# Sliding windows by DMA: thirteen staged batches, one doubled store for each, and the last 15 windows of a copy on GpSimd's ring

## The chip, the core and the metric

The kernel runs on one core of one Trainium2 chip. It uses no compute engine: all of its work is DMA transfers, which the core's 16 DMA engines carry out. Three of the core's queues can issue them: SyncE's (SP), ScalarE's (ACT) and GpSimd's (POOL). A transfer that is issued is cut into packets; each DMA engine holds a ring of waiting packets for each issuing queue. The metric is the device time of the whole program in microseconds (us), as the median of several runs. One further run was profiled; its trace gives the spans, the queues and the single packets.

## The reference

A float32 array `x` of 32 batches x 4096 rows x 256 columns is cut into overlapping windows of 64 rows, one every 32 rows. Each batch gives 127 windows, and each window is written out whole:

```python
n_windows = (length - window_size) // stride + 1      # 127
result = np.zeros((batch, n_windows, window_size, dim), dtype=np.float32)
for i in range(n_windows):
    start = i * stride
    result[:, i] = x[:, start:start + window_size].copy()
```

A block of 32 rows is 32 KB (32,768 bytes), and a batch has 128 such blocks. A window is two neighbouring blocks, 64 KB. Every block but the first and the last of a batch therefore stands in the output twice: as the second half of window p - 1 and as the first half of window p. In the output these two places are neighbours: half-windows 2p - 1 and 2p.

## The kernel before, in words

Batches go one of two ways.

A **direct** batch (20 of 32) is copied from DRAM to DRAM by SP's queue, `copy` (lines 93 to 99): three transfers of 80, 32 and 15 windows (`COPY_PARTS`, line 16). The second number of each pair says into how many packets a 64 KB window is cut: 4 gives packets of 16 KB, 2 gives 32 KB. Source windows overlap, so each block is read twice.

A **staged** batch (12 of 32, the odd ones from 1 to 23, `STAGED`, line 9) goes through SBUF on ScalarE's queue. `load` (line 75) brings its 128 blocks into a tile, one block to a partition, in 16 KB packets. `store` (line 83) then writes the tile out twice, as two transfers: all blocks to the first halves of their windows, then all blocks to the second halves. There are five tiles (`BUFS`), each with a semaphore for "loaded" and one for "stored". ScalarE's order is: load 0, load 1, then for each batch wait for its load, two stores, and before that the next load; a load into a used tile waits for that tile's stores.

Block 0 has no window before it and block 127 none after it. The staged store writes them all the same, into the last half-window of the batch before and the first half-window of the batch after. These neighbours are direct batches, and must put the right contents there afterwards. So a direct batch next to staged ones waits for the stores of both neighbours (`after_store`, line 71) before SP issues its copy. `_order` (line 102) places each of these "tied" batches among the others, about two and a half staged batches behind the one it waits for. Four batches (`EARLY`: 18, 20, 22, 24) are copied at the very beginning instead, so that SP has work while nothing is stored yet. What the staged stores later overwrite in them is mended at the end (lines 151 to 158): seven transfers of one 32 KB half-window each, after the stores in question.

SP then waits for everything and clears its twelve semaphores (lines 159 to 163). Lines 62 and 73 are the helpers that issue a transfer and that wait for a store; in the trace all transfers stand under line 62.

Of the kernel before, what the change touches and what calls it, by code (L numbers as in the profile page):

```python
# [1 line left out]

# [4 lines left out]


STAGED = tuple(range(1, 24, 2))
BUFS = 5  # L10

EARLY = (18, 20, 22, 24)

BLOCK_PARTS = 2

COPY_PARTS = ((80, 4), (32, 2), (15, 4))


class _Geometry:


    def __init__(self, x, out, W, S):
        self.B, self.L, self.D = x.shape
        self.x, self.out = x, out
        self.n_win = (self.L - W) // S + 1
        self.n_blk = self.L // S
        self.blk = S * self.D
        self.win = W * self.D
        assert W == 2 * S and self.n_blk == self.n_win + 1 == 128

    def src(self, b, block, dims):

        at = (b * self.n_blk + block) * self.blk
        return bass.AP(self.x.tensor, self.x.offset + at, dims)

    def dst(self, b, half, dims):

        at = b * self.n_win * self.win + half * self.blk
        return bass.AP(self.out.tensor, self.out.offset + at, dims)

    def rows(self, b, w0, n):

        s, d = [[self.blk, n], [1, self.win]], [[self.win, n], [1, self.win]]
        return self.dst(b, 2 * w0, d), self.src(b, w0, s)

    def half(self, b, half, block):

        dims = [[self.blk // 16, 16], [1, self.blk // 16]]
        return self.dst(b, half, dims), self.src(b, block, dims)


class _Kernel:
    def __init__(self, nc, g, tiles):
        self.nc, self.g, self.tiles = nc, g, tiles
        self.loaded = [nc.alloc_semaphore(f"loaded{i}") for i in range(len(tiles))]
        self.stored = [nc.alloc_semaphore(f"stored{i}") for i in range(len(tiles))]
        self.copied = nc.alloc_semaphore("copied")
        self.early = nc.alloc_semaphore("early")
        self.count = {}

    def start(self, engine, out, in_, sem, parts=1):
        engine.dma_start(out=out, in_=in_, max_dma_last_dim=65536 // parts).then_inc(sem, 16)
        self.count[id(sem)] = self.count.get(id(sem), 0) + 16

    def all_of(self, engine, sem):
        engine.wait_ge(sem, self.count[id(sem)])

    def slot(self, n):
        return divmod(n, len(self.tiles))

    def after_store(self, engine, n):
        turn, i = self.slot(n)
        engine.wait_ge(self.stored[i], 32 * (turn + 1))

    def load(self, n):

        g, (_, i) = self.g, self.slot(n)
        if n >= len(self.tiles):
            self.after_store(self.nc.scalar, n - len(self.tiles))
        src = g.src(STAGED[n], 0, [[g.blk, g.n_blk], [1, g.blk]])  # L80
        self.start(self.nc.scalar, self.tiles[i][:, :], src, self.loaded[i], 2 * BLOCK_PARTS)

    def store(self, n):

        g, (turn, i) = self.g, self.slot(n)
        self.nc.scalar.wait_ge(self.loaded[i], 16 * (turn + 1))
        for half in (0, -1):
            dst = g.dst(STAGED[n], half, [[g.win, g.n_blk], [1, g.blk]])  # L90
            self.start(self.nc.scalar, dst, self.tiles[i][:, :], self.stored[i], 2 * BLOCK_PARTS)

    def copy(self, b, sem):

        w = 0
        for rows, parts in COPY_PARTS:
            self.start(self.nc.sync, *self.g.rows(b, w, rows), sem, parts)
            w += rows
        assert w == self.g.n_win


def _order(B):


    near = {b for s in STAGED for b in (s - 1, s + 1)}
    order = list(EARLY) + [b for b in range(B) if b not in near and b not in STAGED]
    tied = sorted(near - set(EARLY))
    n = len(order) + len(tied)
    for b in tied:
        behind = max(STAGED.index(s) for s in (b - 1, b + 1) if s in STAGED)  # L110
        order.insert(-(-(2 * behind + 5) * n // (2 * len(STAGED))), b)
    return order


@with_exitstack
def kernel(
    ctx: ExitStack,
    tc: tile.TileContext,
    x: bass.AP,
    window_size: bass.AP,  # L120
    stride: bass.AP,
    out: bass.AP,
):
    nc = tc.nc
    W, S = int(window_size), int(stride)
    g = _Geometry(x, out, W, S)
    assert 0 not in STAGED and g.B - 1 not in STAGED
    pool = ctx.enter_context(tc.tile_pool(name="blocks", bufs=1))
    tiles = [pool.tile([g.n_blk, g.blk], x.dtype, name=f"xb{i}") for i in range(BUFS)]

    with tc.tile_critical():
        k = _Kernel(nc, g, tiles)
        for b in _order(g.B):
            if b not in EARLY:
                for s in (b - 1, b + 1):
                    if s in STAGED:
                        k.after_store(nc.sync, STAGED.index(s))
            k.copy(b, k.early if b in EARLY else k.copied)
        k.load(0)
        waited = False  # L140
        last = len(STAGED) - 1
        for n, s in enumerate(STAGED):
            if n < last:
                k.load(n + 1)
            if not waited and (s - 1 in EARLY or s + 1 in EARLY):
                k.all_of(nc.scalar, k.early)
                waited = True
            k.store(n)


        k.all_of(nc.sync, k.early)
        for n, s in enumerate(STAGED):
            if s - 1 in EARLY or s + 1 in EARLY:
                k.after_store(nc.sync, n)
            if s - 1 in EARLY:
                k.start(nc.sync, *g.half(s - 1, 2 * g.n_win - 1, g.n_blk - 1), k.copied)
            if s + 1 in EARLY:
                k.start(nc.sync, *g.half(s + 1, 0, 0), k.copied)
        for n in range(len(STAGED)):
            k.after_store(nc.sync, n)  # L160
        k.all_of(nc.sync, k.copied)
        for sem in [*k.loaded, *k.stored, k.copied, k.early]:
            nc.sync.sem_clear(sem)


# [1 line left out]
_INS = ['x', 'window_size', 'stride']  # L167
_OUTS = [((32, 127, 64, 256), 'float32')]

_NUMBERS = {'window_size': 64, 'stride': 32}  # L170


# [26 lines left out]
```

## Time and profile before

| | us |
|---|---|
| median of 3 runs | 766.62 |
| lowest and highest | 765.39, 766.91 |
| the profiled execution | 768.4 |
| its span | 766.6 |

GpSimd's four MEMSETs (0.2 us in all) are the only engine work in the span. Where each transfer comes from, with the number of transfers, the KB of each and the median time from issue to landing:

```profile
out_dram<-in_x_dram SPq DMA_DIRECT2D x20, 5120.0 KB, 114.8
out_dram<-xb ACTq DMA_DIRECT2D x24, 4096.0 KB, 84.6
xb<-in_x_dram ACTq DMA_DIRECT2D x12, 4096.0 KB, 123.2
out_dram<-in_x_dram SPq DMA_DIRECT2D x20, 2048.0 KB, 116.7
out_dram<-in_x_dram SPq DMA_DIRECT2D x20, 960.0 KB, 97.7
out_dram<-in_x_dram SPq DMA_DIRECT2D x7, 32.0 KB, 48.3
```

The three groups of 20 are the parts of the direct copies (80, 32 and 15 windows), the group of 24 the two stores of each staged batch, the group of 12 the loads, the group of 7 the mends. A landing some 100 us after the issue means that a transfer waits behind others in its ring; it is no measure of how long its own bytes take. In the parts of the profile on the DMA, q1 is SP's queue and q10 ScalarE's; "share" is the time that packets took, as a share of 16 engines' span.

### The profile page before, as it was taken

How to read it: one execution, taken by the hardware profiler on the slowest of the kernel's cores; microseconds unless marked ns; L12 is line 12 of the kernel's file. 1: busy time of each engine (PE TensorE's matmuls, PEld its weight loads, DVE VectorE, ACT ScalarE, POOL GpSimd, SP SyncE). 2: the span in 40 equal slices, each digit the busy share in tenths (PEclk: the TensorE clock that was granted, in tenths of full speed). 3: DMA queues.
4: the chain of work that ended last, by engine and by line, in shares of the span. 5: the costliest groups of instructions: out<-in, count | busy, mean ns of one | idle time of the engine just before them, and what ended most of it. 6: DMA issues, size and time to landing. Idle time of an engine off the chain costs nothing. (4 is left out here: it accounts for less than half of the span.)

```text
span 766.6 us, 180 instructions
## 1 busy us (share of the span) xinstructions
POOL 0.2 (0%) x4
## 2 busy tenths in 40 slices
POOL 0000000000000000000000000000000000000000
DMA  8999999999999999999999999999999999999996
GB/s 371 425 410 421 405 428 431 408 411 427 423 415 421 431 415 425 432 408 416 427 420 417 431 420 420 423 428 410 414 427 419 422 428 418 417 428 421 420 406 237
DMA packets 19837, 317.70 MB, mean 414 GB/s; under 512 B 1628, under 2 KB 1628, under 8 KB 1740
## 3 DMA queue, kind: packets, MB, share of 16 engines
q1 hardware_dynamic: 10044, 166.70, 51.9%
q10 hardware_dynamic: 9792, 151.00, 47.3%
q14 instruction: 1, 0.01, 0.0%
HBM read 217.02 MB, written 267.35 MB: 632 GB/s over the span
## 5 line engine op out<-in xcount | busy, mean ns | idle before, releaser
L180 POOL MEMSET const-bfloat16-1.0<- 128x1 bf16 x1 | 0.1, 102 | 0.0
L180 POOL MEMSET const-uint8-127<- 128x1 uint8 x1 | 0.1, 102 | 0.0
L180 POOL MEMSET const-float32-0.0<- 128x1 f32 x1 | 0.1, 99 | 0.2 <-issue 0.2
L180 POOL MEMSET const-float32-1.0<- 128x1 f32 x1 | 0.1, 99 | 0.0
## 6 DMA issues: line engine op xcount, KB each, us to landing
out_dram<-in_x_dram SPq DMA_DIRECT2D x20, 5120.0 KB, 114.8
out_dram<-xb ACTq DMA_DIRECT2D x24, 4096.0 KB, 84.6
xb<-in_x_dram ACTq DMA_DIRECT2D x12, 4096.0 KB, 123.2
out_dram<-in_x_dram SPq DMA_DIRECT2D x20, 2048.0 KB, 116.7
out_dram<-in_x_dram SPq DMA_DIRECT2D x20, 960.0 KB, 97.7
out_dram<-in_x_dram SPq DMA_DIRECT2D x7, 32.0 KB, 48.3
```

Of the source, the lines that this page charges most:

```text
L180: nc = _bacc.Bacc("TRN2", target_bir_lowering=False, num_devices=1)
```

## The change

Thirteen batches are staged in place of twelve (the odd ones from 1 to 25), and nineteen are direct; the early ones are now 20, 22, 24 and 26. A staged batch is loaded in 32 KB packets. It is stored by one transfer: its source names each partition's block twice (a step of 0), and its destination is the two neighbouring half-windows 2p - 1 and 2p, 64 KB side by side. The last staged batch is stored in three parts, partitions 0 to 31 and 96 to 127 first, which hold the two blocks that spill into the neighbours.

A direct batch is cut into 96 windows in 32 KB packets, 16 windows in 16 KB packets, both on SP's queue, and the last 15 windows in 32 KB packets on GpSimd's queue. GpSimd waits, for each copy, until a load that stands about as far along in its sequence has landed (`paced`), and for a tied batch until its neighbours are stored, as SP does. The mends wait for the early copies on both queues; those beside the last staged batch wait only for its first two parts (`fringe`). At the end GpSimd waits for all semaphores, resets its DMA state and clears them as one range.

```diff
-STAGED = tuple(range(1, 24, 2))
+STAGED = tuple(range(1, 26, 2))
 BUFS = 5
-EARLY = (18, 20, 22, 24)
-BLOCK_PARTS = 2
-COPY_PARTS = ((80, 4), (32, 2), (15, 4))
+EARLY = (20, 22, 24, 26)
+GROUPS = ((96, 2), (16, 4))
+OTHER_PARTS = 2
+SLACK = 1
+LAST = ((0, 32), (96, 32), (32, 64))
...
     def after_store(self, engine, n):
         turn, i = self.slot(n)
-        engine.wait_ge(self.stored[i], 32 * (turn + 1))
+        engine.wait_ge(self.stored[i], 16 * (turn + 1))
...
-        self.start(self.nc.scalar, self.tiles[i][:, :], src, self.loaded[i], 2 * BLOCK_PARTS)
+        self.start(self.nc.scalar, self.tiles[i][:, :], src, self.loaded[i])
-    def store(self, n):
-        g, (turn, i) = self.g, self.slot(n)
-        self.nc.scalar.wait_ge(self.loaded[i], 16 * (turn + 1))
-        for half in (0, -1):
-            dst = g.dst(STAGED[n], half, [[g.win, g.n_blk], [1, g.blk]])
-            self.start(self.nc.scalar, dst, self.tiles[i][:, :], self.stored[i], 2 * BLOCK_PARTS)
+    def store(self, n, p0, rows, sem=None):
+        g, (_, i) = self.g, self.slot(n)
+        tile = self.tiles[i][p0 : p0 + rows, :]
+        src = bass.AP(tile.tensor, tile.offset, [list(tile.ap[0]), [0, 2], [1, g.blk]])
+        dst = g.dst(STAGED[n], 2 * p0 - 1, [[g.win, rows], [g.blk, 2], [1, g.blk]])
+        self.start(self.nc.scalar, dst, src, sem or self.stored[i])
...
+    def copy_others(self, b, sem):
+        w = sum(n for n, _ in GROUPS)
+        self.start(self.nc.gpsimd, *self.g.rows(b, w, self.g.n_win - w), sem, OTHER_PARTS)
...
+def _copies(k):
+    nc, order = k.nc, _order(k.g.B)
+    for c, b in enumerate(order):
+        early = b in EARLY
+        if not early:
+            for n in _beside(b):
+                k.after_store(nc.sync, n)
+        k.copy(b, k.early if early else k.copied)
+        paced = c * len(STAGED) // len(order) - SLACK
+        if paced >= 0:
+            k.after_load(nc.gpsimd, paced)
+        if not early:
+            for n in _beside(b):
+                k.after_store(nc.gpsimd, n)
+        k.copy_others(b, k.early_others if early else k.others)
...
+        if n < last:
+            k.store(n, 0, g.n_blk)
+        else:
+            for p0, rows in LAST:
+                alone = p0 > 0 and p0 + rows < g.n_blk
+                k.store(n, p0, rows, None if alone else k.fringe)
...
+        if n == len(STAGED) - 1:
+            k.all_of(nc.sync, k.fringe)
+        elif s - 1 in EARLY or s + 1 in EARLY:
+            k.after_store(nc.sync, n)
...
+def _end(k):
+    for sem in k.sems:
+        k.all_of(k.nc.gpsimd, sem)
+    k.nc.gpsimd.dma_reset()
+    used = sorted(sem.num for sem in k.sems)
+    k.nc.gpsimd.sem_clear(range(used[0], used[-1] + 1))
```

## The prediction

> **What bounds the kernel now.** No compute engine works: the chain of waits gives 0% to everything, so I read the page's part on the DMA queues first, then its transfers, then stretches of the span, then the sync queue's own waits, and last the trace's packet records.
>
> ```profile
> DMA  8999999999999999999999999999999999999996
> DMA packets 19837, 317.70 MB, mean 414 GB/s; under 512 B 1628, under 2 KB 1628, under 8 KB 1740
> q1 hardware_dynamic: 10044, 166.70, 51.9%
> q10 hardware_dynamic: 9792, 151.00, 47.3%
> HBM read 217.02 MB, written 267.35 MB: 632 GB/s over the span
> ```
>
> The two queues together take 99.2% of 16 engines' span, from the second slice to the last but one. SP's queue (q1) moves the 20 direct copies, ScalarE's (q10) the 12 staged batches. Their bytes check: a direct copy is 127 x 64 KB = 8.32 MB, a staged batch 4.19 MB in and twice 4.19 MB out, 12.58 MB. So a staged batch costs the engines half as much again, and saves only HBM reading.
>
> The packet records (start, length, size and queue of each) say what one engine does. 16 KB packets have a median of 611 ns, 32 KB ones 1213 ns, and on the same engine the next packet begins 3 or 4 ns before the last ends, in over 99% of cases. One 16 KB packet thus holds an engine 607.2 ns, a 32 KB one 1209.2. Linking the packets this way separates the 16 engines: 15 end between 755 and 764 us, one ends at 720.7. That one gets nothing of the 15-row transfers, whose completions come from 15 engines. The stretches near the end show it:
>
> ```profile
> 690.00:720.00 30.00, 0.00 (x0) 1.00 1.01 426
> 720.00:735.00 15.00, 0.00 (x0) 1.00 0.94 401
> 735.00:747.00 12.00, 0.00 (x0) 1.00 0.95 407
> 755.00:760.00 5.00, 0.00 (x0) 1.00 0.75 265
> ```
>
> The last two columns are the DMA share and GB/s: at 720 us a sixteenth disappears. The other loss is seen inside the run:
>
> ```profile
> 108.00:143.00 35.00, 0.00 (x0) 1.00 1.00 428
> 144.00:155.00 11.00, 0.00 (x0) 1.00 1.00 380
> 207.00:233.00 26.00, 0.00 (x0) 1.00 1.01 408
> 233.00:262.00 29.00, 0.00 (x0) 1.00 1.01 434
> ```
>
> Equally busy engines move 434 or 380 GB/s: some packets are long. The means are 622.8 ns (SP, 16 KB, 7600 packets), 628.4 (ScalarE, 16 KB, 9216) and 1252.5 (SP, 32 KB, 1280). Over the medians that is (7600 x 11.8 + 9216 x 17.4 + 1280 x 39.5) ns / 16 = 18.8 us per engine. The long ones cluster while ScalarE's ring loads (4.1% over the median there, 2.6% and 1.6% in the first and second store) and while SP's 32-row group runs.
>
> **The sum for before.** Each of the 15 full engines has 12 x 3 x 16 = 576 packets of 16 KB from ScalarE, and from SP 20 x 24 = 480 of 16 KB and 20 x 4 = 80 of 32 KB: 1056 x 607.2 + 80 x 1209.2 = 737.9 us. Some 100 completion packets at 5 ns and seven 2 KB mend packets at about 0.13 make 1.4. First packet at 2.0, excess 18.8. That is 760.1; the span is 766.6, so 6.5 remain: the slowest engine's lag behind the mean (3.5), the mends landing after the last copies (1.9) and the last 1.8 less overlap. The profiled execution took 768.4, 1.8 around the span; the shown runs have a median of 766.62. I carry the difference over to the median.
>
> **The change, part by part.**
>
> *One batch moves from direct to staged.* Per engine 24 packets of 32 KB come and 127/16 = 7.9 rows of 64 KB go: 29.0 - 19.2 = +9.8 us. HBM reads fall to 212.9 MB, writes stay at 267.4.
>
> *Packet sizes and rings.* ScalarE: 13 x (8 + 16) = 312 of 32 KB per engine. SP: 19 x 12 = 228 of 32 KB and 19 x 4 = 76 of 16 KB. A 32 KB packet saves 5.2 ns over two of 16 KB, some 2.5 us in all. With completions SP has 342 turns and ScalarE 340, so both rings last until the end; and were one dry, the engine would take the other's packet, as the seamless records show.
>
> *The last 15 rows on GpSimd's ring.* 19 x 30 = 570 packets of 32 KB. Before shows no transfer issued there. Bounds: spread evenly, 35.6 per engine, 575.6 x 1209.2 + 76 x 607.2 = 742.2; on the same 15 engines as the nearest row, 38 each, 745.1. I take the middle, 743.6, as the ends lie near each other.
>
> The Trainium skill (DMA: Bandwidth & Descriptors, section "Issuing engines are not separate DMA queues") says that all issuing engines share the same 16 DMA engines, so a further ring saves issue time only; the 99.2% above agrees, and taken alone it leaves 745.1. The same page ("Why a DMA increments its semaphore by 16 and not by 1") says that GpSimd's transfers with k below 16 take k consecutive engines from a rotating cursor; this would give 742.2, and no run here shows it yet.
>
> *The waits.* GpSimd's queue now waits for loads and stores; behind a wait stand only its own later 15-row transfers. The four early ones are out after the second load (landed at 43 us) and are needed at the tenth store, past 450 us; the last is released by load 12 of 13, some 70 us before the end. Cost 0, covered by those margins; if GpSimd were late by more, its 7 us of packets would stand at the end. SP's waits remain:
>
> ```profile
> SPq L62 <- DMA out_dram<-xb: 61.2, 2, 40.2
> SPq L73 <- DMA out_dram<-xb: 19.2, 3, 9.4
> SPq L66 <- DMA out_dram<-in_x_dram: 7.7, 1, 7.7
> ```
>
> They total 88 us on the queue and cost nothing, because a backlog of packets keeps the engines full. SP loses a third transfer per copy and ScalarE one store per batch; issues of 0.4 to 1 us, hidden by the same backlog.
>
> *The end.* The last store goes out in three parts, the two with the fringe first, so the mends can run beside the remaining 8 packets per engine (9.7 us): the 1.9 us go. GpSimd takes over the final clearing with a reset; before shows no such reset. Bounds -1 (twelve clears within the last 1.8 us become one) and +2 (another such end on top); I take 0. Rest: 6.5 - 1.9 = 4.6.
>
> *The excess.* By rows: ScalarE 34.8 ns per 32 KB x 312 = 10.9 us; SP's 228 at 39.5 (its 32 KB row) = 9.0, or at 23.6 (two of its 16 KB rows) = 5.4; 76 x 11.8 = 0.9; GpSimd's 36 in the same way 0.8 to 1.4. So 18.0 to 22.2. If all took SP's 16 KB rate of 1.9%, 14.3. I take 18.0: SP's 32 KB packets ran long where they alternated with 16 KB ones, giving copies two thirds of the engine, and now 32 meets 32.
>
> *Sum:* 2.0 + 743.6 + 1.4 + 18.0 + 4.6 = 769.6, that is 3.0 over 766.6; for the median, 769.6.
>
> **The rivals.**
>
> *The slow packets fade (faster).* For: the 434 GB/s stretches show that hardly any excess is needed when packets of equal size alternate and ScalarE stores, and the changed kernel has equal sizes for three quarters of SP's turns. Against: 13 loads in place of 12, and during 36 turns of GpSimd's ring copies again hold two thirds of an engine, 131 us, about as long as the 32-row groups held before (145). With excess 10 and even spreading: 2.0 + 742.2 + 1.4 + 10.0 + 4.6 = 760.2. It begins to decide below an excess of 15.
>
> *It cancels (no change).* Excess 15 to 17 with even spreading: 765.2 to 767.2.
>
> *The doubled read is slow (much slower).* The store names 128 source rows twice and 256 destination rows, so which engine reads which partition may differ from before, where rows matched one to one, and two engines could meet at one place of SBUF. Place: 208 store packets per engine, 252 us. Against: before's stores are within 2.6% of the median. Price: 2.5 us for each per cent, from 3% on more than all else here; at 5%, 782.
>
> *The ring does not rotate.* It does not do what moving it could do: 745.1, hence 771.1, within the forecast.
>
> **How the numbers follow.** A difference under 0.2%, 1.5 us, can't be told from none. Forecast (768.2 to 777.5: ends by 742.2 + 18.0, and 745.1 + 22.2 with 2 at the end) 0.39; fading 0.36; cancelling 0.13; doubled read 0.12. Slower is 0.39 + 0.12 = 0.51, same 0.13, faster 0.36. The likeliest alone has 768 to 777.5; the range reaches down into the fading case to 759, leaving some 0.1 below, and to 778 above, leaving 0.1.
>
> **What would show it.** Right: some 12,000 packets, 321.9 MB, with 139.7 MB on SP's queue, 163.6 on ScalarE's, 18.7 on a third; 32 KB packets with median 1213 ns; no sixteenth missing after 720 us (or still missing, if the ring does not rotate); mends landing before the last store; mean excess near 18 us. Wrong: a median other than 1213 on any ring, stores above 1280 ns in the mean, stretches in which the DMA share drops below 0.95 before the last 10 us, or a mean rate above 425 GB/s (321.9 MB in 757 us), which would mean that the excess is gone.

## The result and the profile after

The changed kernel is slower: a median of 778.61 us (776.25 to 782.06, 6 runs) against 766.25 us for the kernel before beside it, a ratio of 1.0162 with a 95% interval of 1.0131 to 1.0194. That is 12.4 us; 3.0 had been forecast, and the range ended at 778.0. The profiled execution took 776.49 us (span 774.7) and so lies at the low end of its runs: the profile shows 8.1 us of the 12.4.

The DMA part of the page after (packets, MB and share of 16 engines' span for each queue; q0 is GpSimd's):

```profile
DMA packets 12048, 321.95 MB, mean 416 GB/s; under 512 B 1510, under 2 KB 1510, under 8 KB 1622
q10 hardware_dynamic: 5440, 163.58, 50.4%
q1 hardware_dynamic: 5696, 139.69, 43.2%
q0 software_dynamic: 912, 18.68, 5.7%
HBM read 212.89 MB, written 267.42 MB: 620 GB/s over the span
```

The bytes, packets and HBM traffic are those of the forecast, and the engines are again full (99.3%). The mean rate even rises, from 414 to 416 GB/s, but there are 4.25 MB more to move.

Stretches of the span after (columns: stretch, length, busy GpSimd, TensorE clock, DMA share, GB/s):

```profile
580.00:615.00 35.00, 0.00 (x0) 1.00 1.00 433
668.00:690.00 22.00, 0.00 (x0) 1.00 1.02 413
690.00:726.00 36.00, 0.00 (x0) 1.00 0.99 428
726.00:748.00 22.00, 0.00 (x0) 1.00 1.00 375
748.00:764.00 16.00, 0.00 (x0) 1.00 0.99 428
764.00:768.00 4.00, 0.00 (x0) 1.00 0.88 374
```

No engine is missing after 720 us: the share stays at 1.00 up to 764, where the kernel before had 0.94 from 720 on. A new slow stretch stands at 726 to 748 us, where the first two of the last staged batch's three parts are stored (they land at 738.2 and 750.1 us).

Two transfers of the page's last part, and SP's own waits:

```profile
out_dram<-in_x_dram POOLq DMA_DIRECT2D x19, 960.0 KB, 14.4
out_dram<-in_x_dram SPq DMA_DIRECT2D x7, 32.0 KB, 40.5
```

```profile
SPq L88 <- DMA out_dram<-xb: 508.9, 9, 59.3
SPq L73 <- DMA out_dram<-xb: 202.0, 4, 81.8
```

GpSimd's 15 rows land 14.4 us after the issue; after the first two its issues are 18 us or more apart, so its ring is empty when they come. The mends take 40.5 us: they stand in SP's ring behind its last copies. SP waits 711 us in place of 88, and spends less time on the issues themselves (a median of 0.6 us each in place of 8.1); nothing is lost by it, for the engines stay full.

The same sum as in the prediction, from the packet records of each profiled execution. "Packets" is all packets at 607.2 and 1209.2 ns, as a mean over 16 engines; "excess" is the time by which they ran longer than 611 and 1213 ns, the medians. The rest is what is left of the span when the packets of the full engines and the other rows are taken off:

| us per engine | before | after | forecast |
|---|---|---|---|
| first packet | 2.0 | 1.9 | 2.0 |
| packets, mean of 16 | 734.9 | 742.2 | |
| packets, the full engines | 737.9 | 742.2 | 743.6 |
| excess | 18.8 | 23.2 | 18.0 |
| small packets | 1.4 | 1.0 | 1.4 |
| rest to the span's end | 6.5 | 6.4 | 4.6 |
| span | 766.6 | 774.7 | 769.6 |

### The profile page after: what moved, and what is told of

It is laid out like the page before. It is cut to its first block, busy times and chain, and to the rows that moved or that the text cites. A ratio compares the mean times of both kernels' runs of the same rounds, so it can differ in the third digit from the quotient of the medians.

```text
span 774.7 us, 173 instructions
## 1 busy us (share of the span) xinstructions
POOL 11.3 (1%) x23
## 4 chain that ended last, share of the span: by engine, by line
another core or an unknown queue 74%; DMA 6%; POOL 1%; issue 1%; ACTq 0%; POOLq 0%; SPq 0%
DMA xb<-in_x_dram 6%; POOL out_dram L73 1%; POOLq L88 0%; ACTq L73 0%; ACTq L253 0%; SPq L217 0%
## 5 line engine op out<-in xcount | busy, mean ns | idle before, releaser
L73 POOL DMA_DIRECT2D out_dram<-in_x_dram x19 | 11.1, 584 | 624.5 <-DMA out_dram<-xb 357.4
## 6 DMA issues: line engine op xcount, KB each, us to landing
out_dram<-in_x_dram POOLq DMA_DIRECT2D x19, 960.0 KB, 14.4
out_dram<-in_x_dram SPq DMA_DIRECT2D x7, 32.0 KB, 40.5
```

## The experiments

Each ratio is to the kernel before, run on the same chip beside it. "Packets" is the mean over 16 engines; packets and excess are those of the one profiled execution of each kernel.

| kernel | median us | ratio and interval | packets | excess |
|---|---|---|---|---|
| changed kernel | 778.61 | 1.0162 (1.0131 to 1.0194) | 742.2 | 23.2 |
| e1 12 staged | 785.96 | 1.0219 (1.0191 to 1.0247) | 732.4 | 35.8 |
| e2 last batch whole | 779.22 | 1.0143 (1.0119 to 1.0166) | 742.2 | 21.3 |
| e3 15 rows on SP | 789.74 | 1.0296 (1.0273 to 1.0320) | 742.2 | 29.0 |
| e4 two stores | 782.37 | 1.0207 (1.0179 to 1.0236) | 742.2 | 26.6 |
| e5 12 staged, turns balanced | 771.65 | 1.0047 (1.0029 to 1.0065) | 732.2 | 26.9 |
| e6 staging of before, third ring | 774.54 | 1.0093 (1.0077 to 1.0109) | 734.6 | 26.8 |
| e7 before with 13 staged | 777.24 | 1.0125 (1.0108 to 1.0142) | 744.8 | 17.6 |
| e8 as e4, packets halved | 781.97 | 1.0188 (1.0163 to 1.0213) | 745.4 | 24.2 |
| e9 two rings, balanced | 776.06 | 1.0115 (1.0097 to 1.0134) | 742.0 | 18.9 |
| e10 16 rows on the third ring | 782.14 | 1.0192 (1.0174 to 1.0210) | 742.2 | 25.1 |
| e11 12 staged, two rings | 782.27 | 1.0197 (1.0176 to 1.0218) | 732.9 | 32.0 |
| e12 control of e6, two rings | 770.10 | 1.0031 (1.0019 to 1.0044) | 734.8 | 21.9 |
| e13 bursts in store phases | 779.96 | 1.0147 (1.0124 to 1.0169) | 742.2 | 22.4 |
| e14 e5 with e13 | 770.76 | 1.0050 (1.0032 to 1.0067) | 732.2 | 26.0 |
| e15 e14 with e2 | 768.62 | 1.0023 (1.0015 to 1.0032) | 732.2 | 23.9 |
| e16 before, 15 rows in 32 KB | 770.35 | 1.0045 (1.0033 to 1.0057) | 734.7 | 18.7 |

### The thirteenth batch: e1, e5, e7

```diff
-STAGED = tuple(range(1, 26, 2))
+STAGED = tuple(range(1, 24, 2))
-EARLY = (20, 22, 24, 26)
+EARLY = (18, 20, 22, 24)
```

> The changed kernel with 12 staged batches (odd ones 1 to 23) and the early four 18 to 24; all else as changed. Bytes theory: one batch back to direct gives 24 packets of 32 KB per engine for 7.9 rows, -9.8 us, and one load phase less, -1.3 us of excess: the median falls from 778.6 to about 767.5, span to about 764. Contention theory (the doubled store, 32 KB packets or the third ring make the packets long): the thirteenth batch matters little beyond its share; excess stays at 22 us or more and the median stays above 771. SP then has 20 x 16 packets against ScalarE's 288 per engine, so copies run alone at the end for some 30 turns: if DRAM-to-DRAM alone is slow, 770 or more.

With 9.8 us of packets less, e1 became 7 us slower than the changed kernel by the medians, and 4.4 by the ratios, whose intervals just touch. Its stretches tell where:

```profile
700.00:720.00 20.00, 0.00 (x0) 1.00 1.00 387
720.00:760.00 40.00, 0.00 (x0) 1.00 1.00 326
```

ScalarE's ring was done at 718.7 us. From there the engines, still full, moved 326 GB/s, and 12 of the 35.8 us of excess lie there: a DRAM-to-DRAM copy that has no SBUF transfer beside it runs about a third longer than in company (about 430 GB/s). The last condition of the expectation holds, and the bytes are not the whole price: copies must not be left alone at the end. e5 keeps 12 batches and balances the turns.

```diff
 # e1, and
-GROUPS = ((96, 2), (16, 4))
+GROUPS = ((112, 2),)
```

> The changed kernel with 12 staged batches, and SP's copies cut as 112 rows in 32 KB packets, so that SP's ring has 20 x 15 = 300 turns against ScalarE's 288 + 24 completions = 312; the 15 rows stay on GpSimd's ring. Turn theory (e1 was slow only because ScalarE's ring ran dry 58 us before the end and copies alone move 327 GB/s): both rings end together, packets are 9688 x 1209.2 ns / 16 = 732.2 us per engine, excess about 20, median 764 to 769. Rival (with 12 batches and large packets copies are slow throughout): excess stays above 28 us, median above 773.

At a ratio of 1.0047 it is 8.8 us faster than the changed kernel by their ratios (0.0115 x 767). The turn theory holds so far as no copies are left alone at the end: SP's last copy ends at 749.2 us, ScalarE's last store at 765.2, and beside these stores SP's ring has only the small packets of the mends (to 765.4 us). But the excess, forecast at about 20, was 26.9, and the time is 2.7 us above the forecast's 764 to 769. The same step from the other side puts the batch alone into the kernel before:

```diff
-STAGED = tuple(range(1, 24, 2))
+STAGED = tuple(range(1, 26, 2))
-EARLY = (18, 20, 22, 24)
+EARLY = (20, 22, 24, 26)
```

> The kernel before with the thirteenth staged batch alone (odd ones 1 to 25, early four 20 to 26). Bytes theory: per engine 48 packets of 16 KB more from ScalarE and 28 fewer turns from SP (24 of 16 KB and 4 of 32 KB): 747.7 us in place of 737.9, excess +1.5: median 776 to 779. Contention theory (less copying, less excess; SP's ring ends first and the end is stores alone): excess falls by 4 us or more and the median is 772 or below.

777.24 us, 9.6 us over the kernel before, as the bytes theory had it, though the excess did not rise by 1.5 us but fell by 1.2, to 17.6. Its stretches near the end:

```profile
690.00:720.00 30.00, 0.00 (x0) 1.00 0.99 420
720.00:760.00 40.00, 0.00 (x0) 1.00 0.97 412
```

SP's copies end first here (729.4 us), and the rate holds: by the packet records ScalarE's ring has 97% of the engines' time from 740 to 760 us, at 419 GB/s, and its packets run at their median (611.2 ns in the mean). An end of stores alone costs no excess, an end of copies alone does.

### The third ring: e3, e6, e9, e10, e12

```diff
-        self.start(self.nc.gpsimd, *self.g.rows(b, w, self.g.n_win - w), sem, OTHER_PARTS)
+        self.start(self.nc.sync, *self.g.rows(b, w, self.g.n_win - w), sem, OTHER_PARTS)
```

e3 is this edit, with GpSimd's waits left out.

> The changed kernel with the 15-row transfers on SP's queue again, without GpSimd's waits; packets as changed. Rotation theory: one engine again gets none of them and ends some 45 us early, the other 15 have 38 packets more in place of 35.6: +2.9 us of packets; the median rises to 781 or 782. Third-ring theory (three rings at once cost excess or the rotation costs as much as it gives): excess falls by 3 us or more and the median is 778 or below.

789.74 us, beyond either. SP's ring had got 19 x 21 = 399 turns against ScalarE's 340, so ScalarE's was done at 719.3 us, and copies alone followed, as in e1; one engine was missing besides (the share is 0.94):

```profile
720.00:760.00 40.00, 0.00 (x0) 1.00 0.94 324
```

Its time says nothing on the third ring; e9 repeats it with SP's copies cut as 112 rows (the edit of e5), which makes 342 turns.

> The changed kernel (13 staged, doubled stores, 32 KB) without GpSimd's ring: SP's copies are 112 and 15 rows in 32 KB packets, 19 x 18 = 342 turns against ScalarE's 340, so neither ring runs dry early as in e3. Third-ring theory: the excess falls from 23.2 to 18 or below, and pays for the sixteenth engine's absence (745.1 in place of 742.2 on fifteen): median 772 to 775. Rival (the third ring costs nothing, its rotation is worth 3 us): excess as in the changed kernel, median 781 to 783.

776.06 us, excess 18.9 in place of 23.2: the third-ring theory, a shade above its figures. By the ratios e9 is 3.6 us under the changed kernel, though the two intervals meet at 1.0131 to 1.0134, and the two profiled spans differ by 0.4 us only (774.3 and 774.7). The edit also takes away the 16 KB packets of the 16 rows; they can't be what ran long, for while SP's ring held them the changed kernel's packets ran 2.8% over the median, and 3.2% in the rest of the run. The pair e6 and e12 is clearer in time. e6 stages as the kernel before does and has the third ring:

```diff
 # the changed kernel with e1's edit, LAST = ((0, 128),), loads in 16 KB packets, and
-GROUPS = ((96, 2), (16, 4))
+GROUPS = ((80, 4), (32, 2))
-            k.store(n, 0, g.n_blk)
+            k.store_twice(n)      # two transfers in 16 KB packets, as before
```

> The kernel before in its staging (12 batches, two stores each, 16 KB packets, copies of 80 rows in 16 KB and 32 rows in 32 KB packets), with the 15 rows on GpSimd's ring and the changed kernel's waits and end; the last batch is stored whole. Rotation theory: the sixteenth engine's 45 us are shared out, 734.9 us of packets on every engine in place of 737.9 on fifteen, excess as before (18.8): 3 us off, median about 763 to 764.5. Third-ring theory (three rings at once lengthen packets): excess above 22, median 767 or more.

> The control of e6: the same kernel (12 batches staged as in the kernel before, the changed kernel's waits and end) with the 15 rows on SP's ring in 16 KB packets. Third-ring theory: excess back near 18.8, median 766 to 768.5 as the kernel before, 6 to 8 us under e6's 774.5. Rival (e6 was slow through its waits or its end, not the ring): 772 or more.

774.54 against 770.10 us, 1.0093 against 1.0031 with intervals apart: with the third ring the kernel is 4.8 us slower, although the ring spares it the idle sixteenth engine (3 us). Some 2 us of this are not the ring's: in e6 ScalarE's last store lands last, at 767.9 us, and two mends that wait for it follow, to 770.7. e12 is 1.6 us above its forecast, and its stretches point to the reason: its last store, in 32 KB packets, takes half the turns, and ScalarE's ring ends at 742 us in place of 754.

```profile
700.00:740.00 40.00, 0.00 (x0) 1.00 0.98 417
740.00:760.00 20.00, 0.00 (x0) 1.00 0.94 335
```

So the excess was 21.9, of which 3.1 lie in the phase after ScalarE's last transfer. In e6 it was 26.8 without such a phase, for its copies end at 724.6 us and stores alone follow, whose packets run at their medians:

```profile
720.00:760.00 40.00, 0.00 (x0) 1.00 1.01 428
```

The difference stands against the ring. e6's 15 rows are in 32 KB packets and e12's in 16 KB, but that is not it: e16 below makes the same step in the kernel before, and its excess stays at 18.7.

All runs together say the same. With the phase of copies alone taken off (12.2 us in e1, 10.1 in e3, 3.1 in e12), six kernels with two rings have an excess of 17.6 to 18.9 us, and the eleven with three rings 21.3 to 26.9. Only e11, with two rings and 32.0, stands apart; its packet sizes are dealt with below.

GpSimd's transfers differ from SP's by the ring and by the engines that they use. e10 parts the two: 16 rows on GpSimd's ring (all engines), 15 on SP's.

```diff
-GROUPS = ((96, 2), (16, 4))
+GROUPS = ((96, 2), (15, 4))
```

> The changed kernel with 16 rows on GpSimd's ring and 15 on SP's: the third ring stays, but its transfers now use all 16 engines, and SP's 15-row ones leave one engine out. Third-ring theory: the excess stays at 22 us or more, and the missing sixteenth costs 2.9 us: median 780 to 783. If it is the rotating start that lengthens packets: excess falls by 3 us or more, median 777 or below.

782.14 us, within the forecast; excess 25.1. The ring costs without the rotating start too, and the lost rotation costs another 0.3% (2.3 us, the intervals overlap).

### What about the third ring is slow: e13, e14

Averaged over the loads of the changed kernel, packets that start 9 to 6 and 6 to 3 us before the end of a load's last packets run about 4% and 7% over the median; in e9 it is about 1% and 2%. (These shares, and those of load and store phases below, shift by a point or more with the moment at which a phase is taken to end; the semaphore is up 2 to 3 us after the last packets.) Just before, bursts of GpSimd's ring pass (a tied batch's 15 rows are released by a store's landing, and so fall into the next load). e13 moves these bursts into store phases.

```diff
             for n in _beside(b):
                 k.after_store(nc.gpsimd, n)
+            k.after_load(nc.gpsimd, min(max([paced, *(n + 2 for n in _beside(b))]), len(STAGED) - 1))
```

> The changed kernel with one wait more on GpSimd's queue: a tied batch's 15 rows also wait for the load after next, which lands just as a store phase begins. All bursts of the third ring then stand in store phases. Burst-place theory: load phases fall from 6.0% to about 4.7%, excess from 23.2 to 19 or 20, median 774 to 776. Rival (the third ring's presence lengthens packets wherever its bursts stand): excess stays above 22, median 778 or more.

> e5 (12 staged batches, 112 rows on SP's ring, 15 on GpSimd's) with the bursts in store phases as in e13. Burst-place theory: excess falls from 26.9 by 3 to 5 us, median 767 to 769, even with the kernel before. Rival: as e5, 771 to 772.5.

The place of the long packets moved, the time did not. In e13 the same two steps run about 1% and 3% over the median, and load phases fall from 6.0% to 5.4%; but store phases rise from 1.4% to 1.7%, the spike in the last 3 us of a load from some 13% to some 16%, and the excess is 22.4 in all, the median 779.96 us (776.0 to 780.6). e14 is at 770.76 against e5's 771.65, with overlapping intervals. The burst-place theory falls as an account of the cost: with the bursts elsewhere the excess is about as high. Nor do the long packets stand beside GpSimd's: in the changed kernel only some 4 of the 23.2 us fall into the stretches in which GpSimd's packets are under way. By what mechanism the third ring lengthens the others stays open.

### The stores: e2, e4, e8, e15

```diff
-LAST = ((0, 32), (96, 32), (32, 64))
+LAST = ((0, 128),)
```

> The changed kernel with the last staged batch stored whole by one transfer of 128 partitions, in place of three of 32, 32 and 64; the mends then wait for all of it. Last-store theory: the stretch at 375 GB/s before the end goes, excess falls by 2 to 3 us (from 23.2 to about 20.7), and the mends come back to the end with some 2 us: the median between 776 and 778.6. Rival (the slow stretch is a load phase or chance): no such change, the stretch remains, and the median rises by the mends' 2 us to 780.

The same stretches of e2:

```profile
690.00:726.00 36.00, 0.00 (x0) 1.00 1.01 432
726.00:748.00 22.00, 0.00 (x0) 1.00 1.00 430
748.00:764.00 16.00, 0.00 (x0) 1.00 0.99 415
```

The slow stretch is gone (430 in place of 375 GB/s), ScalarE's packets that start in it are down from 1454 to 1231 ns in the mean, and the excess is 1.9 us lower. Yet the median did not move beyond the spread. It moves a little further in e15, where the edit is made on e14:

> e14 with the last staged batch stored whole. Last-store theory: the slow stretch near the end (11% over the median in e5) goes, 2 us off; the mends come behind it, 1 to 2 us on: within 1 us of e14, 766 to 769. To beat the kernel before it would have to stay under 766.

768.62 us, 2.1 us under e14 (the intervals just meet), and 2.1 us of excess less: the parts of 32 partitions cost about that much. It does not beat the kernel before (1.0015 to 1.0032).

e4 stores each batch but the last by two transfers in 32 KB packets.

```diff
+        for half in (0, -1):
+            dst = g.dst(STAGED[n], half, [[g.win, g.n_blk], [1, g.blk]])
+            self.start(self.nc.scalar, dst, self.tiles[i][:, :], self.stored[i])
```

> The changed kernel with each staged batch but the last stored by two transfers (first halves, then second halves), as before, in 32 KB packets; all else as changed. Doubled-store theory (one transfer that reads a block twice makes longer packets): excess falls by 3 us or more, the median to 775 or below. Rival (the store's form is neutral; the stores' packets are near their median already): within 1.5 us of the changed kernel's 778.6 and the store phases keep an excess near 1.2%.

> The kernel of e4 (two stores) with every packet halved: 16 KB for loads, stores, the 96 rows and GpSimd's 15, 8 KB for the 16 rows; only the last batch's three stores keep 32 KB. The rings keep the proportion of their turns. Packet-size theory (32 KB packets run longer over their median than two of 16 KB): excess falls from e4's 26.6 to 22 or below, the packets cost 3 us more, median 780 or below. Neutral: excess as in e4, median 3 to 4 us above its 782.4.

e4 is slower than the changed kernel by 3.4 us of the ratios, with overlapping intervals: the doubled store does no harm, and may help. ScalarE's packets take 1250.6 ns in the mean in the changed kernel and 1258.7 in e4, and the store phases of the changed kernel have 1.4% of excess, three-part store included. e8 halves e4's packets and is even with it (781.97), between its two forecasts: the excess falls by 2.4 us to 24.2, although 4.1 of that lie in the last store alone, whose 256 packets of 32 KB ran 1471 ns in the mean; the 3.2 us that more packets cost take it back. Packet size by itself does not decide.

### Two more attempts to beat both: e11, e16

e11 stages 12 batches with doubled stores in 32 KB packets, loads in 16 KB, and no third ring; e16 changes `COPY_PARTS` of the kernel before to `((80, 4), (32, 2), (15, 2))`.

> Search for a kernel that beats both: 12 staged batches, doubled stores in 32 KB packets, loads in 16 KB, no third ring; SP's copies 112 rows in 32 KB and 15 in 16 KB packets, 400 turns against ScalarE's 410; last batch stored whole. Packets on fifteen engines 735.9 us against the 737.9 of the kernel before. If the excess is that of the kernel before (18.8): 764 to 766. If 32 KB copies beside 16 KB loads lengthen the packets (load phases above 6%): 770 or more.

> The kernel before with its 15-row transfers in 32 KB packets: SP's turns fall from 620 to 580 per engine, ScalarE's stay at 612, so SP's ring ends first and the last stretch is stores alone. Turn theory: the 10 us of copies alone at the end of the kernel before (its ScalarE ring ends at 754.2, SP's at 763.8) go, 1 to 2 us off, median 765.5 to 766.5. Rival (32 KB copies beside 16 KB packets lengthen them, as its 32-row group does): excess rises by 1 us or more, median 768 or above.

e11's second forecast holds: load phases run 8.1% over the median, against 4.6% in the kernel before. There the copies' 32 KB packets alternate with the loads' 16 KB ones, and take two thirds of the engines. e16 fails: its excess is that of the kernel before (18.7) and the copies alone at the end are gone, yet it takes 770.35 us. Its packet records show what came in their place: ScalarE's last store now ends last, at 764.2 us, and the two mends that wait for it run alone behind it, from 765.9 to 767.2 us; in the kernel before that store landed at 755.3 us, and the mends ran within SP's backlog, to 763.8 us.

## Why the prediction was wrong

**The direction was right, the size was not:** +3.0 was forecast, +12.4 measured. The sum gave 769.6 for the span and for the median; they came to 774.7 and 778.61. It falls short at these terms.

- *The excess: 18.0 forecast, 23.2 in the profile; the failed step.* I took the low end of 18.0 to 22.2, since 32 KB packets would now meet 32 KB ones: SP's 228 packets at 23.6 ns over the median. They ran 43.8 over, beyond the upper bound of 39.5, and ScalarE's 37.6 in place of 34.8; GpSimd's own cost 1.0 us, as forecast. What a third ring does to the packets of the other two had been put at nothing. Without it, in e9, SP's 32 KB packets ran 31.3 ns over and ScalarE's 30.1, and the excess was 18.9: near the forecast, and the third ring adds the other 4.3. The 18.9 include about 2 for the three-part last store (e2, e15), which the sum had left out too. A share for the thirteenth load phase does not show: with the thirteenth batch alone the excess fell (e7). The first rival had named the ring's price only as one of its own difficulties, and weighed it as equal to the 32-row groups that went.
- *The third ring as a whole* stood in the sum at a gain (743.6 where the fifteen engines would have had 745.1) and is a loss: by e9 3.6 us net (intervals that meet), by e6 and e12 4.8, of which some 2 are e6's late mends. The even spreading came: 742.2 us, the share near 1.00 up to 764 us, and 32 to 36 of GpSimd's packets on each engine that can be followed through the run, where always the same fifteen engines would have had 38. This agrees with the Trainium skill (DMA: Bandwidth & Descriptors, section "Why a DMA increments its semaphore by 16 and not by 1"), by which GpSimd's transfers on fewer than 16 engines take consecutive engines from a rotating cursor. The Trainium skill's statement that a further ring only saves issue time (DMA: Bandwidth & Descriptors, section "Issuing engines are not separate DMA queues") spoke against the change; e6 against e12 agrees in that nothing was gained, and goes beyond it, for the ring cost 4.9 us of excess.
- *The rest: 4.6 forecast, 6.4 measured.* The mends were to run beside the last 8 packets of ScalarE. The last four were issued from 729.8 to 750.6 us, 20 to 40 us early, but stood in SP's ring behind the copies, which end last (771.5 us, ScalarE's stores at 769.1): the records have the mends from 764.1 to 772.1 us. In the kernel before it was the same, copies to 763.2 us and mends to 763.8, so there were no 1.9 us to save. Issuing early doesn't put a transfer ahead in its ring. GpSimd's end, taken at 0, was right: from the last landing to the span's end it is 1.7 us, 1.8 before.
- *From the profiled execution to the median.* I carried the kernel before's difference over, and this is 3.9 of the 9.0 us by which the median was missed. The kernel before's profiled execution was 2.1 us above its runs' median, the changed kernel's is 2.1 below, and its runs spread by 5.8 us against 2.4; why they do is not shown.

**Right:** the thirteenth batch's price. +9.8 us of packets were forecast, and e7 measured 9.6 by itself; it is the largest part of the 12.4. Packets, bytes and HBM traffic came as written, the medians of 611 and 1213 ns held on all three rings, and SP's and GpSimd's waits cost nothing that shows. The doubled read did no harm (e4), so that rival falls; the fading and the cancelling of the excess did not come.

**Wrong without effect here:** "were one dry, the engine would take the other's packet". It does, and stays full, but a copy alone runs a quarter to a third longer (32 KB packets of 1520 ns in e3 and 1611 in e1 from 720 to 760 us, against 1213). The changed kernel's two rings end 3 us apart and escaped that. (By its own terms the forecast's upper end is 777.3, not 777.5; nothing hangs on it.)

By the ratios, with 766.25: from the kernel before to the thirteenth batch (e7), +9.6; from there to the packets, doubled stores, three-part last store and end without the third ring (e9 for e7), -0.8; the third ring with the 16 rows in 16 KB packets (changed kernel for e9), +3.6. Together 12.4; only e7's part is measured clear of its neighbours' intervals.

## What to carry to other kernels

Where DMA engines are full, cost a change by what each engine has to move, packet by packet, and then ask what runs beside what: bytes saved are lost again if the slow kind of transfer is left alone at the end (e1 against e5). Count the turns of each ring (packets and completions): the engines alternate between rings by packet, as the records of the two kernels show in over 99% of the places where the next packet of an engine can be told. A transfer that is issued early waits behind its own queue's backlog all the same, and a transfer that waits for the very last store stands alone behind it (e6, e16). Don't count a further ring as free because its own packets are: ask a run what it does to the others.

## What the runs showed of the hardware

- Copies from DRAM to DRAM alone move 326 GB/s with the engines full (e1), and 324 at a share of 0.94 (e3); beside ScalarE's transfers it is 413 to 433 (changed kernel, its slow stretch apart), and with stores from SBUF almost alone 428 GB/s with no excess (e6).
- Two stores of 32 partitions each beside copies: 375 GB/s, against 430 for one store of 128 at the same place (changed kernel and e2).
- A third ring that carries 6% of the bytes adds 4 to 5 us of excess in two pairs of kernels (18.9 to 23.2; 21.9 to 26.8), and its 15-row transfers load the engines evenly (32 to 36 packets on each that can be followed), where on SP's ring one engine gets none of them.
- In four kernels (the kernel before, the changed one, e9, e13) the packets that start in the last 3 us before the end of a load's last packets run about 10 to 18% over the median. No run told why.
